# The FFN of a hybrid diffusion block on one Trainium2 core: the order of the seven block products of a tile, the copies of products ahead on ScalarE, activations stored whole and split when they are read, and x_mix stored one tile later

## Chip, core and metric

One core of a Trainium2 chip runs the whole layer as one program. The metric is the device time of one execution in microseconds (us); lower is better. TensorE (PE) multiplies, VectorE (DVE), ScalarE (ACT) and GpSimd (POOL) do elementwise work, and SyncE (SP) issues the DMAs. Each engine runs its own instructions strictly in order and waits on semaphores for the others. A matmul here multiplies a 128x128 weight block with 128x512 activations.

## The reference, cut to what matters

One layer over 1024 latent tokens of width 1024 with 256 context tokens: modulated RMSNorm, one input projection, three token mixers, a gated merge, and then the part that the change touches:

```python
x_mix = x + m_lat[:, :, 2] * merge_branches(ya, yb, yc, gates, w_branch[l], w_out[l])
h = rms_norm(x_mix, norm_ffn[l]) * (1.0 + m_lat[:, :, 4]) + m_lat[:, :, 3]
x = x_mix + m_lat[:, :, 5] * conv_ffn(h, w_up[l], w_dw[l], b_dw[l], w_down[l])
...
def conv_ffn(h, w_up, w_dw, b_dw, w_down):
    a, g = jnp.split(dwconv(h @ w_up, w_dw, b_dw), 2, axis=-1)   # width 2*2816, 3 taps along the tokens
    return (a * jax.nn.silu(g)) @ w_down
```

All of it is fp32 in and out.

## The kernel before, in words

**Precision.** A product of fp32 matrices is made of three fp32r matmuls: both operands are split into a high part (a cast to fp32r, on ACT) and a low part (the value less its high part, on DVE), and high x high, high x low and low x high are summed in PSUM. The helper `split` (L644) writes such a pair. Weights come in through raw buffers `wr` (3), high parts `wh` (3) and low parts `wl` (3).

**The stages at the end of the program.** `wo_half` (L656) is the output projection, half of the tokens at a time; it makes `xm` (x_mix), stores it to the DRAM tensor `xm_d` (L669) and sums its squares. Then the up projection runs over 22 tiles f of 128 hidden channels; each tile has a value half a and a gate half g. Tiles 0 and 1 are plain products (`plain`). While they run, the operand sums for the other tiles, T1 to T4, are built from `xm` and split (L742 to L757); eight of those sums run on POOL (L748, L752). Tiles 2 to 21 use a Strassen-Winograd scheme: the 2x2 block product (input halves by token halves) with 7 block products in place of 8, 12 matmuls each, 84 in a tile. `w_pair` (L764) loads and splits the weights of a tile, `w_sums` (L778) forms their sums S1 to S4 on POOL and splits them, `up_first` (L804) makes the first two products into the PSUM tile z, and `up_rest` (L812) the other five.

**One tile in up_rest.** The first product, z[:,0], is wanted by itself and as the start of a sum, so ACT copies it to `sn` (p, L815) before PE adds S2·T2 on top of it in the same bank; that sum is copied as u2 (L830). The products S3·T3 (bank c) and S1·T1 (bank d) are likewise copied as p7 (L825) and p5 (L826) before PE adds 22·T4 and S4·22 on top. POOL adds p7 and p5 (L831); DVE makes the four quadrants (L822, L832 to L834). `act_out` (L680) applies the convolution (ACT L692, then DVE L698 and L701, for the gate and for the value), SiLU on ACT (L705), and the product (L708), splits the result into ah and al and stores both parts to `act_d` with two DMAs (L713).

**The down projection** (from L848). Per token half tb and half of the output channels, PE goes through the 22 tiles f: 12 matmuls for each f (`dn`, L863). `act` (L854) loads the split activations, high and low part side by side, from `act_d` into a ring of 27 buffers `ac` (L859). The weights come as 11 units, each for two f.

**What sets the order.** A scheduler places every engine's instructions by program order, dependencies and priorities (`tc.high_priority` moves a piece ahead). The order on each engine is fixed when the program is built. Buffer counts (tag c: NC = 6; s12 and s34: 1) add waits of their own: a buffer is written again only when its last reader is done.

Of the kernel before, what the change touches and what calls it, by code (L numbers as in the profile page):

```python
# [9 lines left out]
F32 = mybir.dt.float32  # L10
F32R = mybir.dt.float32r
# [7 lines left out]
P = 128  # L19
# [15 lines left out]
SKEW = (1, 1)  # L35
APRIO = 60

NC = 6

LAST = (384, 128)  # L40
LPRIO = 40
# [49 lines left out]
def build(tc, ins, out, dbg=None):  # L91
    nc = tc.nc
    V, A, G, T, SP = nc.vector, nc.scalar, nc.gpsimd, nc.tensor, nc.sync
    with ExitStack() as top:
# [18 lines left out]
        def dt_(shape, name, dt=F32):  # L113
            return dp.tile(shape, dt, tag=name, name=name)
# [39 lines left out]
        kv_d = [dt_([10, P, 256], f"kv_d{b}") for b in range(2)]  # L154
        gate_d = dt_([3, KT, P, L], "gate_d")
        xm_d = dt_([2, KT, P, L // 2], "xm_d")
        act_d = dt_([FT, 2, P, 2, L // 2], "act_d")
        y_d = dt_([3, 4, P, L], "y_d")


# [463 lines left out]
        cw = tp.tile([P, 2 * FT, 4], F32, tag="cw", name="cw")  # L624
        SP.dma_start(cw, ins["conv"])

        for nm in ("T1", "T2", "T3"):
            blk[nm] = tuple(tp.tile([P, KQ, LH], F32R, tag=f"{nm}{p}", name=f"{nm}{p}") for p in "hl")
        ffs = ExitStack()
        ff = Aligned(ffs.enter_context(tc.tile_pool(name="ff", bufs=2, reuse_waits="tile")))  # L630
# [24 lines left out]
        def wo_half(hf):  # L655

            cols = slice(hf * LH, hf * LH + LH)
            ss = []
            for i in range(KT):
                w = w_unit(ins["w_out"][i], KT, P)  # L660
                z = bank("b", f"wo{hf}{i}", (P, 512))
                for k2 in range(2):
                    gemm_cm(z, [p[:, k2 * KQ:(k2 + 1) * KQ] for p in w], blk["12"[k2] + "12"[hf]], slice(0, LH),
                            first=k2 == 0, last=k2 == 1)
                xr = ff.tile([P, 512], F32, tag="o", name=f"xr{hf}{i}", bufs=2)
                SP.dma_start(xr, ins["xT"][i * P:(i + 1) * P, cols])
                V.scalar_tensor_tensor(out=xm[i][:, cols], in0=z, scalar=mods[:, 0, i:i + 1], in1=xr,
                                       op0=ALU.mult, op1=ALU.add)
                SP.dma_start(xm_d[hf, i], xm[i][:, cols])  # L669
                sumsq(ff, ss, xm[i][:, cols], i, f"m{hf}", 512, 4)  # L670
            return rms_row(ff, ss, 512, f"m{hf}", "a")

        rp = wo_half(0)
# [9 lines left out]
        def act_out(f, cc_):  # L683

            us = []
            for s in (1, 0):
                c_ = s * FT + f
                u = pc.tile([P, L], F32, tag="c", name=f"u{f}{s}", bufs=NC)
                o = 0
                for z in cc_[s]:  # L690
                    n = z.shape[-1]
                    A.activation(u[:, o:o + n], z, AF.Identity, scale=cw[:, c_, 1:2], bias=cw[:, c_, 3:4])  # L692
                    o += n
                o = 0
                for z in cc_[s]:
                    n = z.shape[-1]
                    e = min(n, L - 1 - o)
                    V.scalar_tensor_tensor(out=u[:, o + 1:o + 1 + e], in0=z[:, :e], scalar=cw[:, c_, 0:1],  # L698
                                           in1=u[:, o + 1:o + 1 + e], op0=ALU.mult, op1=ALU.add)
                    e = 0 if o else 1  # L700
                    V.scalar_tensor_tensor(out=u[:, o + e - 1:o + n - 1], in0=z[:, e:], scalar=cw[:, c_, 2:3],  # L701
                                           in1=u[:, o + e - 1:o + n - 1], op0=ALU.mult, op1=ALU.add)
                    o += n
                if s:
                    A.activation(u, u, AF.Silu)  # L705
                us.append(u)
            g_, a_ = us
            V.tensor_tensor(out=a_, in0=a_, in1=g_, op=ALU.mult)  # L708
            ah = pc.tile([P, L], F32R, tag="c", name=f"ah{f}", bufs=NC)
            al = pc.tile([P, L], F32R, tag="c", name=f"al{f}", bufs=NC)  # L710
            split((ah, al), a_)
            for j, t in enumerate((ah, al)):
                SP.dma_start(act_d[f].rearrange("b p j t -> p j b t")[:, j],  # L713
                             t.bitcast(F32).rearrange("p (b t) -> p b t", b=2))

        def plain(zs, ws, hf, ks):

# [16 lines left out]
        plain([z[:, 1] for z in za], ws, 1, range(KT))  # L734
        act_out(0, [[z.rearrange("p a b -> p (a b)")] for z in za])
        ws = up_units(1)
        za = [[bank(t, f"up1{s}{hf}", (P, LH)) for hf in range(2)] for s, t in enumerate("ab")]
        for s in range(2):
            for hf in range(2):
                plain([za[s][hf]], [ws[s]], hf, range(KT))  # L740

        t1, t2 = slice(0, LH), slice(LH, L)  # L742
        for k in range(KQ):
            h1, h2 = xm[k], xm[k + KQ]
            b = {nm: [p[:, k] for p in blk[nm]] for nm in ("T1", "T2", "T3")}
            V.tensor_tensor(out=h1[:, t1], in0=h1[:, t2], in1=h1[:, t1], op=ALU.subtract)
            split(b["T1"], h1[:, t1])
            G.tensor_tensor(out=h1[:, t2], in0=h2[:, t2], in1=h1[:, t2], op=ALU.subtract)  # L748
            split(b["T3"], h1[:, t2])
            V.tensor_tensor(out=h2[:, t2], in0=h2[:, t2], in1=h1[:, t1], op=ALU.subtract)  # L750
            split(b["T2"], h2[:, t2])
            G.tensor_tensor(out=h2[:, t1], in0=h2[:, t1], in1=h2[:, t2], op=ALU.subtract)  # L752
        act_out(1, za)

        blk["T4"] = blk["12"]
# [55 lines left out]

        def up_rest(f, z, w):  # L812
            p1 = P1[0]
            sn = p1.tile([P, LH], F32, tag="sn", name=f"p1_{f}", bufs=2)
            A.copy(sn, z[:, 0])  # L815
            prod(z[:, 0], w["S2"], blk["T2"], first=False)
            c = bank("a", f"upc{f}", (P, LH))
            prod(c, w["S3"], blk["T3"])
            d = bank("b", f"upd{f}", (P, LH))
            prod(d, w["S1"], blk["T1"])  # L820
            ca, cg = (pc.tile([P, L], F32, tag="c", name=f"c{s}{f}", bufs=NC) for s in range(2))
            V.tensor_tensor(out=ca[:, t1], in0=z[:, 1], in1=sn, op=ALU.add)  # L822
            p5 = ca[:, t2]
            p7 = cg[:, t2]
            A.copy(p7, c)  # L825
            A.copy(p5, d)  # L826
            prod(c, w["22"], blk["T4"], first=False)
            prod(d, w["S4"], blk["22"], first=False)
            u2 = p1.tile([P, LH], F32, tag="sn", name=f"u2_{f}", bufs=2)
            A.copy(u2, z[:, 0])  # L830
            G.tensor_tensor(out=cg[:, t2], in0=p7, in1=p5, op=ALU.add)  # L831
            V.tensor_tensor(out=cg[:, t2], in0=cg[:, t2], in1=u2, op=ALU.add)  # L832
            V.tensor_tensor(out=cg[:, t1], in0=c, in1=u2, op=ALU.add)  # L833
# [13 lines left out]

        pa = Aligned(top.enter_context(tc.tile_pool(name="pa", bufs=1, side="right", reuse_waits="tile")))  # L848
        p2 = Aligned(top.enter_context(tc.tile_pool(name="p2", bufs=1, reuse_waits="tile")))
        NRING = 27  # L850
        NRIGHT = 16
        acts = {}

        def act(tb, f):  # L854
            if (tb, f) not in acts:
                j = (tb * FT + f) % NRING
                t = (pa if j < NRIGHT else p2).tile([P, 2, LH], F32, tag=f"ac{j}", name=f"ac{tb}_{f}")
                with tc.high_priority(offset=APRIO):
                    SP.dma_start(t, act_d[f, tb])  # L859
                acts[tb, f] = tuple(t[:, j].bitcast(F32R) for j in range(2))  # L860
            return acts[tb, f]

        def dn(z, w, c, h, s, e):  # L863
# [629 lines left out]
```

## Time and profile before

| what | us |
|---|---|
| median of 3 runs (lowest, highest) | 2213.57 (2213.42, 2218.39) |
| the profiled execution's own time | 2217.27 |
| its span in the profile | 2215.5 |
| PE busy in the span | 2100.2 (95%) |
| DVE, ACT, POOL busy | 1465.1, 1002.2, 463.5 |

A row of the timeline gives the start, the duration, the engine, the source line, the operation and its tiles (buffer numbers left out), and in brackets how long the engine sat idle before it and who released it. Matmuls overlap, so PE counts as busy when it starts one each 0.23 us and each lasts 0.39 us; a wait of PE shows as a gap between two starts. PEclk is the granted share of TensorE's full clock. Times are from the start of the span; the up projection of tiles 2 to 21 runs from 1527 to 1946 us.

### The profile page before, as it was taken

Reading aid. Unit: us, or ns where it says so; the run is one execution under the profiler, and the core shown is the slowest. Engines: PE = TensorE matmul, PEld = TensorE weight load, DVE = VectorE, ACT = ScalarE, POOL = GpSimd, SP = SyncE. Lnnn points to the kernel's source line nnn. Section 1 sums busy time; section 2 is a strip of 40 time slices with the busy share of each in tenths; the row PEclk is TensorE's granted clock in tenths of the full one; section 3 lists DMA queues with packets and bytes.
Section 4 is the critical chain, followed back from the end, with each engine's and each line's share of the span. In section 5 each row is a group of like instructions: output and inputs, shape, how many; then the busy total and the mean of one; then the engine's idle time right before and its main releaser. Section 6 shows DMA issues by size and latency. Waiting matters only on the chain. (4 is left out here: it accounts for less than half of the span.)

```text
span 2215.5 us, 31104 instructions
## 1 busy us (share of the span) xinstructions
PE 2100.2 (95%) x11690; PEld 1739.3 (79%) x11690; DVE 1465.1 (66%) x2563; ACT 1002.2 (45%) x1789; POOL 463.5 (21%) x398
## 2 busy tenths in 40 slices
PE   7789999999999999999999999998999999999997
PEld 3778788789988888877777788877777777778887
DVE  6946566637565778599999757569777777732233
ACT  4523333311122777677777634355445445422222
POOL 1420010000021222133323100115443343200010
PEclk9999999999999999999999999999999999999999
DMA  7420111126644211211000454541333223297442
GB/s 307 128 66 30 49 39 34 53 97 190 200 141 128 88 45 51 89 34 32 32 32 27 145 180 150 165 143 67 105 111 108 96 105 105 90 351 281 161 126 91
DMA packets 102871, 247.67 MB, mean 112 GB/s; under 512 B 10944, under 2 KB 36032, under 8 KB 101696
## 3 DMA queue, kind: packets, MB, share of 16 engines
q1 hardware_dynamic: 102432, 245.62, 33.1%
q8 instruction: 92, 1.51, 0.3%
q14 instruction: 59, 0.48, 0.1%
q10 hardware_dynamic: 288, 0.07, 0.0%
HBM read 188.49 MB, written 57.15 MB: 111 GB/s over the span
## 5 line engine op out<-in xcount | busy, mean ns | idle before, releaser
L175 DVE TENSOR_TENSOR wl<-wr,wh 128x1024 fp32r<-128x1024 f32 x147 | 185.2, 1261 | 285.0 <-ACT wh L174 283.4
L174 ACT CAST wh<-wr 128x1024 fp32r<-128x1024 f32 x152 | 158.5, 1044 | 456.5 <-PE dn L865 109.7
L1236 DVE TENSOR_TENSOR pl<-pp,ph 128x512 fp32r<-128x512 f32 x236 | 158.7, 683 | 9.7 <-ACT ph L1235 8.4
L189 PE MATMUL gz<-hh,wh 128*128 128x512 f32 x384 | 156.4, 408 | 3.6 <-ACT gs L486 3.6
L1235 ACT CAST ph<-pp 128x512 fp32r<-128x512 f32 x236 | 136.1, 584 | 43.6 <-PE pp L1231 40.4
L191 PE MATMUL gz<-hh,wl 128*128 128x512 f32 x384 | 151.8, 396 | 0.0
L190 PE MATMUL gz<-hl,wh 128*128 128x512 f32 x384 | 151.6, 395 | 0.0
L200 PE MATMUL tm<-wl,hh 128*128 128x256 f32 x384 | 108.9, 284 | 2.3 <-DVE wl L175 2.3
L199 PE MATMUL tm<-wh,hh 128*128 128x256 f32 x384 | 108.7, 283 | 0.0
L201 PE MATMUL tm<-wh,hl 128*128 128x256 f32 x384 | 108.7, 283 | 0.0
L864 PE MATMUL dn<-ac,wh 128*128 128x512 f32 x264 | 104.0, 394 | 4.5 <-DMA ac<-act_d 4.5
L1225 PE MATMUL po<-ph,VHL 128*128 128x512 f32 x236 | 105.0, 445 | 1.3 <-ACT ph L1235 1.3
L1226 PE MATMUL po<-pl,VHL 128*128 128x512 f32 x236 | 98.9, 419 | 7.6 <-DVE pl L1236 7.3
L866 PE MATMUL dn<-ac,wl 128*128 128x512 f32 x264 | 103.5, 392 | 0.0
L865 PE MATMUL dn<-ac,wh 128*128 128x512 f32 x264 | 103.3, 391 | 0.0
L692 ACT ACTIVATE u<-c,cw 128x1024 f32<-128x1024 f32 x40 | 49.8, 1246 | 96.8 <-DVE c L833 64.8
L1231 PEld LDWEIGHTS pp<-ident,plat 128*128 128x128 f32 x512 | 61.2, 140 | 34.4 <-DVE pl L1236 22.0
L1231 PE MATMUL pp<-ident,plat 128*128 128x128 f32 x512 | 78.2, 275 | 10.3 <-DVE pl L1236 10.1
L189 PEld LDWEIGHTS gz<-hh,wh 128*128 128x128 f32 x384 | 72.8, 189 | 17.8 <-ACT gs L486 5.7
L783 POOL TENSOR_TENSOR s<-wr 128x512 f32<-128x512 f32 x20 | 42.6, 2128 | 200.7 <-DVE ws12l L646 11.5
L191 PEld LDWEIGHTS gz<-hh,wl 128*128 128x128 f32 x384 | 72.5, 189 | 15.3
L190 PEld LDWEIGHTS gz<-hl,wh 128*128 128x128 f32 x384 | 72.8, 190 | 11.5
(1496 smaller groups left out, 6286.3 us busy)
## 6 DMA issues: line engine op xcount, KB each, us to landing
wr<-in_w_cm SPq DMA_DIRECT2D x56, 512.0 KB, 3.6
wr<-in_w_up SPq DMA_DIRECT2D x44, 512.0 KB, 3.5
ac<-act_d SPq DMA_DIRECT2D x44, 512.0 KB, 6.2
wr<-in_w_down SPq DMA_DIRECT2D x33, 512.0 KB, 3.8
wmr<-in_w_mod SPq DMA_DIRECT2D x32, 512.0 KB, 4.8
gate_d<-gs SPq DMA_DIRECT2D x48, 256.0 KB, 2.3
sgt<-gate_d SPq DMA_DIRECT2D x24, 512.0 KB, 3.3
act_d<-ah SPq DMA_DIRECT2D x22, 512.0 KB, 2.9
```

Source lines behind the costliest of these rows:

```text
L174: A.copy(hi[:, :n], raw[:, :n])
L175: (lo_eng or V).tensor_tensor(out=lo[:, :n], in0=raw[:, :n], in1=hi[:, :n].bitcast(F32), op=ALU.subtract)
L189: T.matmul(psl, wh[:, k, c], hh[:, k0 + k, cols], start=s, stop=False)
L190: T.matmul(psl, wh[:, k, c], hl[:, k0 + k, cols], start=False, stop=False)
L191: T.matmul(psl, wl[:, k, c], hh[:, k0 + k, cols], start=False, stop=e)
L199: T.matmul(psl, hh[:, k, toks], wh[:, k % 4, :], start=s, stop=False)
L200: T.matmul(psl, hh[:, k, toks], wl[:, k % 4, :], start=False, stop=False)
L201: T.matmul(psl, hl[:, k, toks], wh[:, k % 4, :], start=False, stop=e)
L1225: T.matmul(po, vv, ph, start=n == 0, stop=False)
L1231: T.transpose(pp[:, h], PT(h, n), ident)
L1235: A.copy(ph, pp)
L1236: V.tensor_tensor(out=pl, in0=pp, in1=ph.bitcast(F32), op=ALU.subtract)
```

## The change

In `up_rest` the seven products come in the order z0, z1, S3·T3, S1·T1, S2·T2, 22·T4, S4·22; the four copies go through `keep`, with a scheduling priority of 30. `act_out` stores the fp32 activations once, whole, and `act` loads half a row set of 128x512 into one of four buffers `st` and splits it there into the ring, which has 25 places. The eight POOL sums go to DVE. Tile 1 makes its gate first. Tag c has 5 buffers. T3 is the first of the T tiles in its pool. The store of `xm` for tile i is written after the sum for tile i+1. The first activation load is written ahead of the loop over tb.

```diff
-NC = 6
+NC = 5
+KPRIO = 30
...
-        act_d = dt_([FT, 2, P, 2, L // 2], "act_d")
+        act_d = dt_([FT, P, L], "act_d")
...
-        for nm in ("T1", "T2", "T3"):
+        for nm in ("T3", "T1", "T2"):
...
-                SP.dma_start(xm_d[hf, i], xm[i][:, cols])
+                if i > 0:
+                    SP.dma_start(xm_d[hf, i - 1], xm[i - 1][:, cols])
...
+            SP.dma_start(xm_d[hf, KT - 1], xm[KT - 1][:, cols])
...
-            ah = pc.tile([P, L], F32R, tag="c", name=f"ah{f}", bufs=NC)
-            al = pc.tile([P, L], F32R, tag="c", name=f"al{f}", bufs=NC)
-            split((ah, al), a_)
-            for j, t in enumerate((ah, al)):
-                SP.dma_start(act_d[f].rearrange("b p j t -> p j b t")[:, j],
-                             t.bitcast(F32).rearrange("p (b t) -> p b t", b=2))
+            SP.dma_start(act_d[f], a_)
...
-        za = [[bank(t, f"up1{s}{hf}", (P, LH)) for hf in range(2)] for s, t in enumerate("ab")]
-        for s in range(2):
+        za = [[bank(t, f"up1{s}{hf}", (P, LH)) for hf in range(2)] for s, t in enumerate("ba")]
+        for s in (1, 0):
...
-            G.tensor_tensor(out=h1[:, t2], in0=h2[:, t2], in1=h1[:, t2], op=ALU.subtract)
+            V.tensor_tensor(out=h1[:, t2], in0=h2[:, t2], in1=h1[:, t2], op=ALU.subtract)
...
-            G.tensor_tensor(out=h2[:, t1], in0=h2[:, t1], in1=h2[:, t2], op=ALU.subtract)
+            V.tensor_tensor(out=h2[:, t1], in0=h2[:, t1], in1=h2[:, t2], op=ALU.subtract)
...
+            def keep(out, src):
+                with tc.high_priority(offset=KPRIO):
+                    A.copy(out, src)
+
             sn = p1.tile([P, LH], F32, tag="sn", name=f"p1_{f}", bufs=2)
-            A.copy(sn, z[:, 0])
-            prod(z[:, 0], w["S2"], blk["T2"], first=False)
+            keep(sn, z[:, 0])
             c = bank("a", f"upc{f}", (P, LH))
             prod(c, w["S3"], blk["T3"])
+            keep(p7, c)
+            V.tensor_tensor(out=ca[:, t1], in0=z[:, 1], in1=sn, op=ALU.add)
             d = bank("b", f"upd{f}", (P, LH))
             prod(d, w["S1"], blk["T1"])
...
+            keep(p5, d)
+            prod(z[:, 0], w["S2"], blk["T2"], first=False)
+            u2 = p1.tile([P, LH], F32, tag="sn", name=f"u2_{f}", bufs=2)
+            keep(u2, z[:, 0])
             prod(c, w["22"], blk["T4"], first=False)
             prod(d, w["S4"], blk["22"], first=False)
...
-        NRING = 27
+        NRING = 25
...
-                t = (pa if j < NRIGHT else p2).tile([P, 2, LH], F32, tag=f"ac{j}", name=f"ac{tb}_{f}")
+                t = (pa if j < NRIGHT else p2).tile([P, 2, LH], F32R, tag=f"ac{j}", name=f"ac{tb}_{f}")
                 with tc.high_priority(offset=APRIO):
-                    SP.dma_start(t, act_d[f, tb])
-                acts[tb, f] = tuple(t[:, j].bitcast(F32R) for j in range(2))
+                    raw = p2.tile([P, LH], F32, tag="st", name=f"st{tb}_{f}", bufs=4)
+                    SP.dma_start(raw, act_d[f][:, tb * LH:(tb + 1) * LH])
+                    acts[tb, f] = (t[:, 0], t[:, 1])
+                    split(acts[tb, f], raw)
...
+        act(0, 0)
```

Every later line has a number of its own in the changed file. On ACT, in tile 10 as in every tile from 4 to 19, these instructions stood in a row before (ws11h and vhS_11 are high parts of the weight sums of tile 11, wa12h of the weights of tile 12; p, u and c are the copies of products):

```order
L705 ACTIVATE u_16085<-u_16085 128x1024
L645 CAST ws11h<-s_11_16255 128x1024
L815 COPY p_10_16156<-up_16131 128x512
L645 CAST ah_16095<-u_16090 128x1024
L830 COPY u_10_16225<-up_16131 128x512
L645 CAST vhS_11_16273<-s_11_16256 128x512
L825 COPY c_16197<-upc_16170 128x512
L645 CAST wa12h<-wr_16393 128x1024
L826 COPY c_16196<-upd_16183 128x512
```

On ACT at the same place now:

```order
L708 ACTIVATE u_16040<-u_16040 128x1024
L646 CAST ws11h<-s_11_16200 128x1024
L818 COPY p_10_16108<-up_16081 128x512
L646 CAST vhS_11_16218<-s_11_16201 128x512
L818 COPY c_16107<-upc_16110 128x512
L818 COPY c_16106<-upd_16125 128x512
L646 CAST wa12h<-wr_16333 128x1024
L818 COPY u_10_16151<-up_16081 128x512
```

The cast ah is gone, the copies of c and d stand ahead of wa12h, and u, which is now made later by PE, stands behind it; p is still behind ws11h.

On DVE in the same tile, before (al is the low part of the activations, ws11l of the weight sums):

```order
L708 TENSOR_TENSOR u_16090<-u_16090,u_16085 128x1024
L646 TENSOR_TENSOR ws11l<-s_11_16255,ws11h 128x1024
L646 TENSOR_TENSOR al_16096<-u_16090,ah_16095 128x1024
L822 TENSOR_TENSOR c_16196<-up_16131,p_10_16156 128x512
L646 TENSOR_TENSOR vlS_11_16274<-s_11_16256,vhS_11_16273 128x512
L646 TENSOR_TENSOR wa12l<-wr_16393,wa12h 128x1024
L832 TENSOR_TENSOR c_16197<-c_16197,u_10_16225 128x512
```

And on DVE now:

```order
L711 TENSOR_TENSOR u_16045<-u_16045,u_16040 128x1024
L647 TENSOR_TENSOR ws11l<-s_11_16200,ws11h 128x1024
L825 TENSOR_TENSOR c_16106<-up_16081,p_10_16108 128x512
L647 TENSOR_TENSOR vlS_11_16219<-s_11_16201,vhS_11_16218 128x512
L647 TENSOR_TENSOR wa12l<-wr_16333,wa12h 128x1024
L835 TENSOR_TENSOR c_16107<-c_16107,u_10_16151 128x512
```

Only al has gone; POOL's five instructions of a tile stand in one and the same order in both.

On SP, where the up projection ends and the down projection begins, before (ah_17847 and al_17848 are tile 21's activations, ac_0 to ac_8 the ring, xt the loads of x_mix):

```order
L171 DMA wr_18044<-in_w_down 128x1024
L859 DMA ac_0_17880<-act_d 128x1024
L859 DMA ac_1_17894<-act_d 128x1024
L859 DMA ac_2_17914<-act_d 128x1024
L859 DMA ac_3_17928<-act_d 128x1024
L859 DMA ac_4_17948<-act_d 128x1024
L713 DMA act_d<-ah_17847 128x2x512
L713 DMA act_d<-al_17848 128x2x512
L859 DMA ac_5_17962<-act_d 128x1024
L859 DMA ac_6_17982<-act_d 128x1024
L893 DMA xt_17863<-xm_d 128x512 x8
```

And on SP now (u_17737 is tile 21's activations):

```order
L172 DMA wr_17964<-in_w_down 128x1024
L712 DMA act_d<-u_17737 128x1024
L865 DMA st_0_17754<-act_d 128x512
L865 DMA st_1_17788<-act_d 128x512
L865 DMA st_2_17811<-act_d 128x512
L865 DMA st_3_17828<-act_d 128x512
L901 DMA xt_17758<-xm_d 128x512
L865 DMA st_4_17851<-act_d 128x512
L901 DMA xt_17758<-xm_d 128x512 x7
L865 DMA st_5_17868<-act_d 128x512
```

Five activation loads stood ahead of the last tile's stores; now the first load stands behind the last tile's store. In the stretch of `wo_half`, the DMAs on SP (weights, xr, xm_d) stand in the same sequence in both programs.

## Rows read from the trace of the kernel before

**Rows 1.** The windows view: the first 50 us of the down projection. Columns: busy us of PE, PEld (weight load), DVE, ACT and POOL with the number of instructions, granted clock, share of the DMA engines, GB/s.
```profile
1950.00:2000.00 50.00, 47.33 (x201) 38.36 (x200) 14.73 (x13) 10.53 (x11) 0.00 (x0) 0.97 0.87 335
```

**Rows 2.** The view of waits of PE between 1540 and 1940 us (the wait for c in tile 2, 0.7 us, left out): who was waited for, us in total, times, longest.
```profile
PE up L801 <- ACT p L815: 22.0, 18, 2.4
PE upc L801 <- ACT vhS L645: 6.7, 1, 6.7
```

**Rows 3.** The timeline of PE in tile 10: its first matmul, and the two around the wait.
```profile
1701.60 0.39 PE L801 MATMUL up<-B11h,wa10h 128*128 128x512 f32 x1
...
1708.40 0.39 PE L801 MATMUL upc<-T3h,vhS 128*128 128x512 f32 x1
1709.94 0.50 PE L801 MATMUL up<-T2h,ws10h 128*128 128x512 f32 x1 [1.16 <-ACT p L815]
```

**Rows 4.** The timeline of ACT in tile 10: the cast of the weight sums, the copy p, the cast ah, and the cast of S4 (vhS).
```profile
1708.38 1.03 ACT L645 CAST ws11h<-s 128x1024 fp32r<-128x1024 f32 x1
1709.31 0.58 ACT L815 COPY p<-up 128x512 f32<-128x512 f32 x1
1711.80 1.05 ACT L645 CAST ah<-u 128x1024 fp32r<-128x1024 f32 x1 [1.91 <-DVE u L708]
...
1715.23 0.62 ACT L645 CAST vhS<-s 128x512 fp32r<-128x512 f32 x1
```

**Rows 5.** The timeline of DVE from one low part of the weight sums (ws11l) to the next (ws12l).
```profile
1711.68 1.22 DVE L646 TENSOR_TENSOR ws11l<-s,ws11h 128x1024 fp32r<-128x1024 f32 x1
1712.88 1.23 DVE L646 TENSOR_TENSOR al<-u,ah 128x1024 fp32r<-128x1024 f32 x1
...
1715.88 1.30 DVE L646 TENSOR_TENSOR vlS<-s,vhS 128x512 fp32r<-128x512 f32 x1 [1.17 <-ACT vhS L645]
1717.71 1.93 DVE L646 TENSOR_TENSOR wa12l<-wr,wa12h 128x1024 fp32r<-128x1024 f32 x1 [0.52 <-ACT wa12h L645]
1722.07 0.69 DVE L832 TENSOR_TENSOR c<-c,u 128x512 f32<-128x512 f32 x1 [2.43 <-POOL c L831]
...
1732.18 1.22 DVE L646 TENSOR_TENSOR ws12l<-s,ws12h 128x1024 fp32r<-128x1024 f32 x1
```

**Rows 6.** The timeline of POOL in the same stretch.
```profile
1713.03 2.23 POOL L783 TENSOR_TENSOR s<-wr 128x512 f32<-128x512 f32 x1 [11.49 <-DVE ws11l L646]
1715.35 1.29 POOL L784 TENSOR_TENSOR s<-s,wr 128x512 f32<-128x512 f32 x1
1717.27 1.29 POOL L789 TENSOR_TENSOR s<-wr,wr 128x512 f32<-128x512 f32 x1 [0.63 <-DVE vlS L646]
1718.52 2.27 POOL L790 TENSOR_TENSOR s<-wr,s 128x512 f32<-128x512 f32 x1
1720.75 1.28 POOL L831 TENSOR_TENSOR c<-c,c 128x512 f32<-128x512 f32 x1
```

**Rows 7.** The chain that ended last, followed back through 1700 to 1725 us: shares of that stretch by engine and line.
```profile
by line: POOL s L790 17.9%; DVE u L698 15.1%; DVE u L701 10.3%; POOL c L831 10.0%; ACT u L692 10.0%; issue 9.5%; DVE c L832 5.5%; DVE vlS L646 5.3%; POOL s L789 5.2%; DVE c L833 4.9%; DVE ws11l L646 4.9%; DVE al L646 4.8%; ACT vhS L645 2.5%
```

**Rows 8.** The timeline of PE at the start of tile 2: the last matmul of the first two products, the one behind the wait, and the end of the slower matmuls that follow.
```profile
1532.34 0.39 PE L803 MATMUL up<-B21h,wa2l 128*128 128x512 f32 x1
1539.44 0.80 PE L801 MATMUL upc<-T3h,vhS 128*128 128x512 f32 x1 [6.72 <-ACT vhS L645]
...
1545.66 0.39 PE L803 MATMUL up<-T2h,ws2l 128*128 128x512 f32 x1
```

**Rows 9.** The timelines of DVE, where the T tiles are built, and of ACT at the start of tile 2.
```profile
1503.28 1.77 DVE L646 TENSOR_TENSOR T2l<-xm,T2h 128x512 fp32r<-128x512 f32 x1
...
1530.83 0.79 ACT L692 ACTIVATE u<-up,cw 128x512 f32<-128x512 f32 x1
1537.34 1.06 ACT L705 ACTIVATE u<-u 128x1024 f32<-128x1024 f32 x1 [5.73 <-DVE u L701]
```

**Rows 10.** The timeline of PE: the last matmul ahead of the wait for p in tiles 4 and 20, and the last matmul of tile 21 with the first of the down projection.
```profile
1585.48 0.39 PE L801 MATMUL upc<-T3h,vhS 128*128 128x512 f32 x1
...
1913.66 0.39 PE L801 MATMUL upc<-T3h,vhS 128*128 128x512 f32 x1
...
1946.01 0.39 PE L803 MATMUL upd<-B22h,vlS 128*128 128x512 f32 x1
1948.27 0.50 PE L864 MATMUL dn<-ac,wh 128*128 128x512 f32 x1 [1.87 <-DMA ac<-act_d]
```

**Rows 11.** The timeline of DVE at the end of tile 21: the quadrant that the gate starts from, and the last product.
```profile
1944.87 0.68 DVE L833 TENSOR_TENSOR c<-upc,u 128x512 f32<-128x512 f32 x1
...
1952.89 1.23 DVE L708 TENSOR_TENSOR u<-u,u 128x1024 f32<-128x1024 f32 x1
```

**Rows 12.** The timeline of PE in the first tiles of the down projection: a wait for an activation load, and the matmuls behind it.
```profile
1967.96 0.39 PE L866 MATMUL dn<-ac,wl 128*128 128x512 f32 x1
1970.57 0.50 PE L864 MATMUL dn<-ac,wh 128*128 128x512 f32 x1 [2.22 <-DMA ac<-act_d]
...
1975.48 0.39 PE L866 MATMUL dn<-ac,wl 128*128 128x512 f32 x1
```

**Rows 13.** DMA issues: KB of each and median us from issue to landing, for the stores of activations and the loads of x by half rows.
```profile
act_d<-ah SPq DMA_DIRECT2D x22, 512.0 KB, 2.9
...
xr<-in_xT SPq DMA_DIRECT2D x16, 256.0 KB, 3.3
```

**Rows 14.** Time from issue to landing, least, median and most, of the ring loads ac.
```profile
DMA to landing us min/median/max: 4.5/6.2/10.6
```

More of the change, by code (lines that the diff above doesn't have):

```diff
@@ L813, in up_rest @@
             p1 = P1[0]
+            ca, cg = (pc.tile([P, L], F32, tag="c", name=f"c{s}{f}", bufs=NC) for s in range(2))
+            p5 = ca[:, t2]
+            p7 = cg[:, t2]
+            def keep(out, src):
+                with tc.high_priority(offset=KPRIO):
+                    A.copy(out, src)
             sn = p1.tile([P, LH], F32, tag="sn", name=f"p1_{f}", bufs=2)
-            A.copy(sn, z[:, 0])
-            prod(z[:, 0], w["S2"], blk["T2"], first=False)
+            keep(sn, z[:, 0])
             c = bank("a", f"upc{f}", (P, LH))
             prod(c, w["S3"], blk["T3"])
+            keep(p7, c)
+            V.tensor_tensor(out=ca[:, t1], in0=z[:, 1], in1=sn, op=ALU.add)
             d = bank("b", f"upd{f}", (P, LH))
             prod(d, w["S1"], blk["T1"])
[L821 to L826, printed above, removed]
+            keep(p5, d)
+            prod(z[:, 0], w["S2"], blk["T2"], first=False)
+            u2 = p1.tile([P, LH], F32, tag="sn", name=f"u2_{f}", bufs=2)
+            keep(u2, z[:, 0])
             prod(c, w["22"], blk["T4"], first=False)
             prod(d, w["S4"], blk["22"], first=False)
-            u2 = p1.tile([P, LH], F32, tag="sn", name=f"u2_{f}", bufs=2)
-            A.copy(u2, z[:, 0])
             G.tensor_tensor(out=cg[:, t2], in0=p7, in1=p5, op=ALU.add)
@@ L855, in act @@
             if (tb, f) not in acts:
-                j = (tb * FT + f) % NRING
-                t = (pa if j < NRIGHT else p2).tile([P, 2, LH], F32, tag=f"ac{j}", name=f"ac{tb}_{f}")
+                n = tb * FT + f
+                j = n % NRING
+                t = (pa if j < NRIGHT else p2).tile([P, 2, LH], F32R, tag=f"ac{j}", name=f"ac{tb}_{f}")
                 with tc.high_priority(offset=APRIO):
-                    SP.dma_start(t, act_d[f, tb])
-                acts[tb, f] = tuple(t[:, j].bitcast(F32R) for j in range(2))
+                    raw = p2.tile([P, LH], F32, tag="st", name=f"st{tb}_{f}", bufs=4)
+                    SP.dma_start(raw, act_d[f][:, tb * LH:(tb + 1) * LH])
+                    acts[tb, f] = (t[:, 0], t[:, 1])
+                    split(acts[tb, f], raw)
             return acts[tb, f]
```

## The prediction

> **What bounds the kernel now.** I read the waits of PE first. In the up projection PE waits 18 times for ACT's copy p, 22.0 us in all, and once 6.7 us for a weight cast [rows 2]. So PE is the engine that loses time; the question is what makes p late. The timeline of PE gives the pitch: 30 matmuls from 1701.60 to 1708.40, 0.2267 us each, and then a gap in front of the first matmul that needs p [rows 3]. From the seventh S3·T3 matmul of tile 4 to that of tile 20 are 328.18 us [rows 10], 20.51 us a tile, where 84 matmuls need 84 x 0.2267 = 19.04.
>
> ACT shows why p is late: it stands behind the cast ws11h [rows 4], which stands behind the post-processing of the tile before. The chain of waits through 1700 to 1725 us then shows what really paces a tile: there is POOL, DVE and ACT in it and no PE [rows 7]. It is a loop. When ws11l ends on DVE (1712.90), POOL may write the weight sums of the next tile, five instructions from 1713.03 to 1722.03 [rows 6]; the last is the sum p7+p5, for which L832 waits; L832, the convolution and the product follow on DVE and ACT up to ws12l, 20.50 us after ws11l [rows 5]. POOL and DVE hardly overlap in it: POOL's L783 takes 2.23 us where L784 takes 1.29, and al runs on DVE meanwhile; DVE's vlS and wa12l take 1.30 and 1.93 beside L784 and L789, where ws11l of the same width as wa12l takes 1.22 [rows 5, 6]. So PE's wait for p is the sign, and this loop is the bound.
>
> The Trainium skill (SBUF — State Buffer, "Practical consequences" in its part on the shared pair) says that a DVE instruction with two SBUF inputs and a GpSimd instruction that reads SBUF exclude each other, whoever issues first. The trace agrees (2.23 against 1.29 us). By that rule a new order inside the loop saves nothing and only work taken out counts; without it the loop would end below 19.04 and PE would set the pace, which is rival A.
>
> **The sum before.** Tile 2's first matmul starts 23 x 0.2267 before 1532.34, at 1527.13; tile 21's last at 1946.01 [rows 8, 10]. 1679 steps of 0.2267 are 380.6 us, 418.9 were taken: 38.3 us lost. Of these, 6.9 is the wait in tile 2 (7.10 less one step) and 2.8 the slow matmuls behind it (15 steps in 6.22 us instead of 3.40: the lower of the two clock levels) [rows 8]; 328.2 - 16 x 19.04 = 23.5 is tiles 4 to 19; 5.1 is the rest of tiles 2, 3 and 20.
>
> **Part by part.** *No split in act_out.* Every tile loses ah (1.05 on ACT) and al (1.2 on DVE, start to start) [rows 4, 5]. ACT is idle 1.91 us ahead of ah, so its loss is worth nothing by itself. al lies in the loop. It cannot give less than what it adds to L783, 2.23 - 1.29 = 0.94, nor more than its own 1.2; vlS no longer queues behind it and u on ACT, so I take 1.1. The loop becomes 20.5 - 1.1 = 19.4, still 0.36 above PE.
>
> *The order of the products.* S2·T2 comes after S1·T1, so PE needs p 24 matmuls (5.4 us) after z, not 7; the waits for p go, as far as the loop lets them. What is late next is the loop itself, 0.36 us a tile; PE meets it again at p, after the little lead that the new order gives. In 17 tiles (4 to 20): 6.1 us lost instead of 23.5 and tile 20's share. I count no gain for the order beyond that. The copies of c and d stand ahead of wa12h, which needs S2·T2 done anyway: nothing. Tag c with 5 buffers adds a wait: copy c overwrites what the value's convolution of the tile before reads, which is done before ws11l starts (1711.68). The copy's turn is after p and vhS, 1709.9 + 0.6, so ACT waits 1.2 us at most, with d, wa12h and u behind it; PE wants c only after 12 more matmuls (2.7 us): nothing.
>
> *Tiles 1 and 2.* vhS, for which PE waited 6.7 us, stands behind the SiLU of tile 1, which waited 5.73 for DVE [rows 2, 9]. Now the gate is made first, 48 matmuls (10.9 us) ahead of tile 1's end, and vhS follows the last convolution start: 1527.3 + 0.79 + 0.62 = 1528.7, its low part some 2.8 later (three half-tile steps of 0.7 and itself); PE needs that at 1533. The eight sums moved to DVE cost 8 x 0.68 = 5.4 there, but a DVE instruction next to a POOL sum takes 1.77 instead of 0.68 [rows 9], 1.1 each, and two al (2.4) go: a gain on DVE, not a loss. I take 1.0 us lost in tiles 2 and 3 together; bounds 0 and what is lost today. Total lost 7.1, so the up projection **gains 31.2 us**.
>
> *x_mix.* In the order SP's sequence is the same in `wo_half`: nothing either way.
>
> *Stores and loads.* act_d is written once and read in half the bytes. The splits come back in the down projection: per f a cast of 0.62 and a subtraction of 0.68, with half a weight unit (0.52 and 0.61) 1.15 on ACT and 1.3 on DVE against 12 x 0.2267 = 2.72 on PE; both engines are mostly idle there [rows 1]. PE hides them, except for the first f.
>
> *The seam.* Today five loads stand ahead of tile 21's stores on SP, and PE starts the down projection 2.26 us after tile 21's last matmul [rows 10]. Now the first load stands behind tile 21's store. That store waits for the product: from L833 to the end of L708 are 9.25 us [rows 11], and L833 can start when 22·T4 is done, 12 steps less 0.4 before the last matmul's start (-2.25; it was -1.1), so the product is ready at +7.0, and store and load are issued one behind the other. The load's landing takes 2.9 to 6.2 us (a 512 KB store; the ring loads' median); the nearest row is xr, 256 KB in half rows, 3.3; I take 4.0, since the store is in flight ahead of it [rows 13, 14]. Cast 0.62: first matmul at +11.6, 11.4 us lost. After 6.7 us of idleness the clock cost 2.8 [rows 8]; I take that again: 14.2. Today the same stretch loses 2.0 at the start, 2.4 in a later wait for a load and 1.7 behind it (14 steps in 4.91 us instead of 3.17) [rows 10, 12]: 6.1. Those waits go with half the bytes. The seam **costs 8.1 us** more.
>
> Sum: -31.2 + 8.1 = -23.1. Against the profiled execution (2217.27, span 2215.5) that is 2194.2; that one lies 3.7 above the median of the runs shown, so against 2213.57 I predict **2190.5**. Its own bounds: al 0.94 to 1.2 (2.7 us up, 1.7 down), landing 2.9 to 6.2 (-1.1, +2.2), tiles 2 and 3 up to 4 more: 2188 to 2199.
>
> **Rivals.** *A. PE becomes the bound* at 19.04 a tile, if the loop falls below that. For: vlS's cast stands ahead of the copies now. Against: POOL's and DVE's instructions still exclude each other. Lost 1.0 instead of 7.1: 2184.5.
>
> *B. The wait at tile 2 stays*, since DVE has 5.4 us more and is full there. Against: the stretched rows [rows 9]. 9.7 comes back: 2200.
>
> *C. Slower: the down projection starves.* Four raw buffers, and a load waits on SP for the split of the fourth before it, with weight loads behind it. A round is 6.2 + 0.62 + 0.68 = 7.5 us for four f, which PE uses in 10.9; the longest landing, 10.6 [rows 14], makes 11.9 and a wait. A wait costs 2.4 + 1.7 = 4.1 us with the clock [rows 12]. Six such waits cancel the gain; from eight on the kernel is slower by over 0.3%. Every second f of the first pass, eleven, would give 2236. Against: half the bytes. The Trainium skill (Perfetto Trace Analysis, "DMA Optimizations") speaks for it: runs of 2 KB instead of 4 KB move less per time. The row for such runs here, xr, is not slow (3.3 us for 256 KB).
>
> *D. Little is left:* B, with two to four waits of C: 2208 to 2217.
>
> **How the numbers follow.** Chances: forecast 0.52, A 0.16, B 0.17, D 0.08, C 0.07. The likeliest gives 2190.5. The range 2178 to 2206 holds the forecast, A and B with their bounds and leaves out C and D. A difference of 0.3% (6.6 us) is about what a measurement of this kernel tells from none: faster 0.85, same 0.08, slower 0.07.
>
> **What would show it.** The steps between the same matmuls of tiles 4 and 20: 19.4 us (19.04 speaks for A, 20 or more against the loop). POOL's L783 near 1.3 us. No wait of PE over 2 us in tile 2. One gap of 11 to 12 us between tile 21 and the down projection, slow matmuls behind it, and then no wait for loads. Wrong would be: the loop as long as before though al is gone, or waits of PE for `ac` all through the first pass.

## The result and the profile after

| | median us | range, runs | profiled execution, span |
|---|---|---|---|
| before | 2213.49 | 2212.89 to 2218.39, 4 | 2217.27, 2215.5 |
| after | 2192.26 | 2190.67 to 2193.44, 4 | 2193.44, 2191.7 |

After over before is 0.9899, with a 95% interval of 0.9882 to 0.9916: 21.2 us less, where 2190.5 was forecast.

The waits of PE between 1530 and 1930 us, to be held against [rows 2]: the 18 waits for p and the one for vhS are gone. What is left is the seam (the passage from tile 21 to the down projection), and small waits for L825, the sum z1+p on DVE.

```profile
PE dn L871 <- ACT ac L646: 11.8, 1, 11.8
PE up L799 <- DVE c L825: 3.3, 3, 1.6
```

The timeline of DVE over one round, from ws11l to ws12l, answers to [rows 5]; that of POOL in the same stretch to [rows 6].

```profile
1694.19 1.22 DVE L647 TENSOR_TENSOR ws11l<-s,ws11h 128x1024 fp32r<-128x1024 f32 x1
1695.33 0.68 DVE L825 TENSOR_TENSOR c<-up,p 128x512 f32<-128x512 f32 x1
1695.93 1.45 DVE L647 TENSOR_TENSOR vlS<-s,vhS 128x512 fp32r<-128x512 f32 x1
1699.97 2.15 DVE L647 TENSOR_TENSOR wa12l<-wr,wa12h 128x1024 fp32r<-128x1024 f32 x1 [2.59 <-ACT wa12h L646]
1703.30 0.69 DVE L835 TENSOR_TENSOR c<-c,u 128x512 f32<-128x512 f32 x1 [1.18 <-POOL c L834]
...
1713.40 1.22 DVE L647 TENSOR_TENSOR ws12l<-s,ws12h 128x1024 fp32r<-128x1024 f32 x1
```

```profile
1695.54 1.29 POOL L781 TENSOR_TENSOR s<-wr 128x512 f32<-128x512 f32 x1 [11.49 <-DVE ws11l L647]
1696.91 1.62 POOL L782 TENSOR_TENSOR s<-s,wr 128x512 f32<-128x512 f32 x1
1698.49 1.29 POOL L787 TENSOR_TENSOR s<-wr,wr 128x512 f32<-128x512 f32 x1
1699.74 1.29 POOL L788 TENSOR_TENSOR s<-wr,s 128x512 f32<-128x512 f32 x1
1700.99 2.27 POOL L834 TENSOR_TENSOR c<-c,c 128x512 f32<-128x512 f32 x1
```

The round is 1713.40 - 1694.19 = 19.21 us instead of 20.50. POOL's first sum takes 1.29 instead of 2.23 us, since al no longer runs beside it, and the gap of 0.63 us ahead of the third sum is gone.

The chain of waits through 1685 to 1710 us holds PE alone, where [rows 7] held no PE:

```profile
by line: PE up L799 18.6%; PE up L800 18.2%; PE up L801 18.1%; PE upd L800 8.2%; PE upc L799 8.2%; PE upd L801 8.1%; PE upc L800 7.3%; PE upd L799 7.3%; PE upc L801 7.2%
```

That reads as if PE set the pace now. It doesn't yet: 84 matmuls need 19.04 us. The missing 0.17 us a tile are split over short steps at the first S2·T2 matmul (1696.06 to 1696.41), too short to be listed as a wait (the run e10_sum_dve settles this).

The timeline of PE from tile 21 into the down projection answers to the last two rows of [rows 10]:

```profile
1915.35 0.39 PE L801 MATMUL upd<-B22h,vlS 128*128 128x512 f32 x1
1927.56 0.80 PE L871 MATMUL dn<-ac,wh 128*128 128x512 f32 x1 [11.82 <-ACT ac L646]
1928.29 0.79 PE L872 MATMUL dn<-ac,wh 128*128 128x512 f32 x1
...
1931.87 0.50 PE L871 MATMUL dn<-ac,wh 128*128 128x512 f32 x1
1932.20 0.39 PE L872 MATMUL dn<-ac,wh 128*128 128x512 f32 x1
```

The timelines of DVE, SP and ACT there, in this order: the product, the store and the loads behind it, the first casts.

```profile
1921.08 1.22 DVE L711 TENSOR_TENSOR u<-u,u 128x1024 f32<-128x1024 f32 x1
...
1922.33 0.33 SPq L712 DMA_DIRECT2D act_d<-u  x1
1922.75 2.20 SPq L865 DMA_DIRECT2D st<-act_d  x4
...
1926.89 1.26 ACT L646 CAST ac<-st 128x512 fp32r<-128x512 f32 x2 [7.54 <-DMA st<-act_d]
```

The product is ready 6.95 us after the last matmul's start, the first load's cast begins 4.1 us after its issue, the first matmul comes at +12.2: one line of waiting, link by link. From 1915.35 to 1932.20 are eleven steps, 2.5 us at 0.2267; they took 16.85, so the seam loses 14.4 us. Later in the down projection PE waits for no load.

### The profile page after: what moved, and what is told of

Its sections match the earlier page's. It is cut to its first block, busy times and chain, and to the rows that moved or that the text cites. A ratio compares the mean times of both kernels' runs of the same rounds, so it can differ in the third digit from the quotient of the medians.

```text
span 2191.7 us, 31143 instructions
## 1 busy us (share of the span) xinstructions
PE 2095.4 (96%) x11690; PEld 1737.6 (79%) x11690; DVE 1467.9 (67%) x2593; ACT 1007.5 (46%) x1811; POOL 440.4 (20%) x390
## 5 line engine op out<-in xcount | busy, mean ns | idle before, releaser
L871 PE MATMUL dn<-ac,wh 128*128 128x512 f32 x264 | 103.9, 393 | 11.8 <-ACT ac L646 11.8
L191 PEld LDWEIGHTS gz<-hl,wh 128*128 128x128 f32 x384 | 72.8, 190 | 11.6
L781 POOL TENSOR_TENSOR s<-wr 128x512 f32<-128x512 f32 x20 | 30.7, 1534 | 231.7 <-DVE ws2l L647 21.5
```

The lines of the kernel that those rows point to most:

```text
L191: T.matmul(psl, wh[:, k, c], hl[:, k0 + k, cols], start=False, stop=False)
L871: T.matmul(z, w[0][:, c], h[0], start=s, stop=False)
```

## The experiments

Each kernel was timed beside the kernel before, whose medians were 2212.6 to 2213.4 in these runs. "Ratio" is to the kernel before, with its 95% interval. A median holds the whole program, also parts that no change here touches: in these traces the 500th matmul starts between 104.1 and 107.8 us, and the last one of `wo_half` between 1476.4 and 1482.3. So the last column gives, from the one trace of each run, the time from the last matmul of `wo_half` to the end of the span; it is 735.0 us in the kernel before and 711.3 in the changed kernel.

| run | median us, runs | ratio | round us | behind `wo_half` us |
|---|---|---|---|---|
| e1_order_alone | 2207.79, 10 | 0.9976 (0.9967 to 0.9986) | 20.13 | 726.2 |
| e2_whole_alone | 2202.31, 6 | 0.9956 (0.9942 to 0.9969) | 19.57 | 723.2 |
| e3_dve_op | 2207.11, 10 | 0.9971 (0.9962 to 0.9981) | 20.08 | 725.3 |
| e4_act_op | 2192.03, 4 | 0.9906 (0.9891 to 0.9920) | | 710.3 |
| e5_gate_last | 2193.36, 4 | 0.9911 (0.9896 to 0.9926) | | 713.9 |
| e7_sums_pool | 2197.95, 4 | 0.9931 (0.9916 to 0.9946) | | 717.5 |
| e6_xm_now | 2190.85, 4 | 0.9902 (0.9887 to 0.9917) | | 710.5 |
| e8_seam_cw | 2185.39, 4 | 0.9876 (0.9860 to 0.9893) | | 706.8 |
| e9_seam_early | 2185.31, 4 | 0.9879 (0.9864 to 0.9894) | | 704.4 |
| e10_sum_dve | 2181.63, 4 | 0.9862 (0.9847 to 0.9876) | 19.04 | 703.0 |
| e12_seam_pool | 2183.32, 4 | 0.9861 (0.9842 to 0.9880) | | 703.5 |
| e13_first_pool | 2177.22, 5 | 0.9833 (0.9819 to 0.9846) | | 698.0 |

### What paces a tile

The theory: the loop ws_l, POOL's five instructions, convolution, product, ws_l. The rival: PE asked for p too early, and the new order of the products gave the gain.

**e1_order_alone**: the kernel before with the change's `up_rest` (the new order and `keep`), nothing else.

> The kernel before, with only the new order of the block products and the early copies on ScalarE; the split in act_out, its two stores, six buffers of tag c and the old loads stay. Loop theory (a tile lasts as long as the round ws_l, POOL sums, convolution, product, ws_l, and al stands in that round): the round stays at 20.3 to 20.5 us, PE's wait only moves to another matmul, and the median falls by 0 to 6 us, to 2207 to 2213. Rival (PE lost its time because it asked for the copy p 7 matmuls after z, and the new order mended that): the tile falls to 19.1 to 19.4 us and the median by 20 to 30, to 2183 to 2193.

5.6 us less: the theory's branch by the median, but the round of 20.13 lies below the 20.3 that it allowed, so the order does give something in the loop. PE's wait moved, as expected: from p to later copies on ACT (L821, 8.9 us in 11 waits) and to L828, this kernel's sum z1+p (8.8 us in 6). The wait of 6.7 us for vhS in tile 2 stands unchanged. Its timeline of POOL, and of DVE at both ends:

```profile
1688.14 2.21 POOL L784 TENSOR_TENSOR s<-wr 128x512 f32<-128x512 f32 x1 [11.49 <-DVE ws10l L647]
1690.43 1.62 POOL L785 TENSOR_TENSOR s<-s,wr 128x512 f32<-128x512 f32 x1
1692.01 1.29 POOL L790 TENSOR_TENSOR s<-wr,wr 128x512 f32<-128x512 f32 x1
...
1686.79 1.22 DVE L647 TENSOR_TENSOR ws10l<-s,ws10h 128x1024 fp32r<-128x1024 f32 x1
...
1706.92 1.22 DVE L647 TENSOR_TENSOR ws11l<-s,ws11h 128x1024 fp32r<-128x1024 f32 x1
```

The first sum still collides with al (2.21), but the third follows without the gap of 0.63 us of [rows 6].

**e2_whole_alone**: the changed kernel with the old `up_rest`, nothing else.

> The changed kernel with the old order of the block products and the old places of the copies; whole store, split when read and all the rest stay. Loop theory: without al the round is 19.2 to 19.5 us whatever the order of the products, but PE asks for p after 7 matmuls instead of 24 and the copies wait longer, so some tenths per tile may come back: 0 to 8 us above the changed kernel, 2192 to 2200. Rival (the order gave the gain): the tile is at 20 us or more, 15 to 25 us above the changed kernel, 2207 to 2217.

10 us above the changed kernel by the median, 12.0 by the last column: between the two branches. Its timelines, as in e1:

```profile
1700.02 1.29 POOL L781 TENSOR_TENSOR s<-wr 128x512 f32<-128x512 f32 x1 [11.49 <-DVE ws11l L647]
1701.39 1.30 POOL L782 TENSOR_TENSOR s<-s,wr 128x512 f32<-128x512 f32 x1
1703.32 1.30 POOL L787 TENSOR_TENSOR s<-wr,wr 128x512 f32<-128x512 f32 x1 [0.63 <-DVE vlS L647]
...
1698.67 1.22 DVE L647 TENSOR_TENSOR ws11l<-s,ws11h 128x1024 fp32r<-128x1024 f32 x1
...
1718.24 1.22 DVE L647 TENSOR_TENSOR ws12l<-s,ws12h 128x1024 fp32r<-128x1024 f32 x1
```

Here the collision is gone and the gap is back. So each half of the change shortened the same stretch of POOL, in a different place. The round of five kernels, cut at the same three events:

| us | before | e1 | e2 | after | e3 |
|---|---|---|---|---|---|
| ws_l starts to POOL's first sum | 1.35 | 1.35 | 1.35 | 1.35 | 1.36 |
| that to DVE's first step that needs POOL's fifth | 9.04 | 8.68 | 8.11 | 7.76 | 8.61 |
| that to the next ws_l | 10.11 | 10.10 | 10.11 | 10.10 | 10.11 |
| round | 20.50 | 20.13 | 19.57 | 19.21 | 20.08 |

Only the middle line moves. Taking al out is worth 0.93 there (before to e2) or 0.92 (e1 to after); the order is worth 0.36 or 0.35; they add up. "The order" is here the whole new `up_rest`: the sequence of the products and the priority of the copies changed together, and neither was tried without the other. Over the 17 tiles the order's share in e2 is 6.0 us; longer waits in tiles 2 and 3 (6.2 us instead of 3.1, with slow matmuls behind the longest) and at the seam (12.6 instead of 11.8) make up the rest.

**e3_dve_op** and **e4_act_op**: a stand-in for al alone, and one for ah alone.

```diff
             SP.dma_start(act_d[f], a_)
+            if 2 <= f < FT - 1:      # e3; in e4: A.copy(g_, a_)
+                V.tensor_tensor(out=g_, in0=a_, in1=g_, op=ALU.subtract)
```

> The changed kernel with one more DVE instruction in tiles 2 to 20: a subtraction of the same width and the same two SBUF inputs as al, in the place that al had behind ws_l, into the dead gate tile; nothing is stored from it. Loop theory: 1.0 to 1.2 us in each of 19 tiles, the round from 19.2 to 20.2 to 20.4, POOL's first sum (L781 of the changed kernel) back from 1.29 to 2.2 us, 18 to 23 us above the changed kernel: 2210 to 2215. Rival (PE sets the pace of the changed kernel, or DVE's idle time swallows the instruction): 0 to 3 us.

14.9 us above the changed kernel, 17 x 0.87 = 14.8: the theory, its size taken too high (18 to 23). The first sum:

```profile
1681.82 2.14 POOL L783 TENSOR_TENSOR s<-wr 128x512 f32<-128x512 f32 x1 [11.49 <-DVE ws10l L647]
```

An instruction of 1.22 us on DVE costs 0.87 us, by making POOL wait: the length that it adds to its neighbour, not its own.

> The changed kernel with one more ACT instruction in tiles 2 to 20: a copy as wide as the cast ah that the change took out, behind the copy p, into the dead gate tile; nothing is stored from it. Loop theory: ACT has idle time there and the instruction is not in the round: within 2 us of the changed kernel, 2190 to 2195. Rival (ACT's queue, in which p stood behind other work, was the bound): 10 to 20 us more.

2192.03: an ACT instruction of the same width (1.05 us, in tiles 2 to 20) costs nothing, as the theory has it.

### The start of tile 2, and x_mix

**e5_gate_last** (tile 1's value half first again) and **e7_sums_pool** (the two sums of the T loop back on `G`) take one edit each out of the change.

> The changed kernel with the value half of tile 1 computed first again, as before (banks a, b and the order of s). By the prediction's step on tile 2 (the wait of 6.7 us went because the gate's SiLU no longer comes last): the wait at tile 2's third product comes back by 3 to 7 us, with the slow matmuls behind it 3 to 9 us above the changed kernel, 2195 to 2201. Rival (it went because DVE was relieved, of al twice and of waiting for POOL's sums): 0 to 2 us.

1.1 us more by the median, less than the two intervals can tell apart; 2.6 more by the last column. PE's waits in the first tiles:

```profile
PE up L799 <- DVE c L825: 4.8, 1, 4.8
PE upc L799 <- ACT vhS L646: 1.2, 1, 1.2
```

Of the 6.7 us for vhS only 1.2 are back, and tile 3's wait for L825 is 4.8 us instead of 1.5. The prediction's reason for tile 2, the gate made first, carries a small part of what was put on it.

> The changed kernel with the eight T sums that the change moved to DVE back on POOL. If DVE was held up by POOL's sums at tile 2 (1.77 us for an instruction that takes 0.68 alone): DVE comes 2 to 6 us later to tile 1's convolution and tile 2 waits that much longer, 2194 to 2200. If not: within 2 us of the changed kernel, or 1 to 3 faster since DVE has 8 x 0.68 us less to do.

5.7 us more (6.3 by the last column), in the first branch's range but not by its way: no wait for vhS came back. The timeline of ACT while the T tiles are built, and of PE behind it:

```profile
1504.80 0.62 ACT L646 CAST T3h<-xm 128x512 fp32r<-128x512 f32 x1 [2.23 <-POOL xm L746]
...
1508.77 1.04 ACT L175 CAST wh<-wr 128x1024 fp32r<-128x1024 f32 x1
...
1509.87 0.79 PE L190 MATMUL up<-B11h,wh 128*128 128x512 f32 x1 [3.61 <-ACT wh L175]
```

ACT waits for POOL's sums, and a weight cast that PE needs for tile 1's gate stands behind it: a place that the prediction did not name. The kernel before has this cast as late, and PE does not wait for it, since the value half comes first there:

```profile
1508.51 1.05 ACT L174 CAST wh<-wr 128x1024 fp32r<-128x1024 f32 x1
```

So the sums on DVE mend what the gate's new place would cost; e7 does not show that they gain anything over the kernel before.

**e6_xm_now**: each x_mix tile stored at once.

> The changed kernel with each x_mix tile stored at once again. By the prediction the store one tile later is worth nothing: within 1.5 us of the changed kernel, 2191 to 2194. Rival (the store held the next load of x on SP and with it the convolution input): 2 to 6 us more.

2190.85, no difference by the intervals (0.8 us less by the last column): worth nothing, as forecast.

### The seam, and a faster kernel

**e8_seam_cw**:

```diff
-            SP.dma_start(act_d[f], a_)
+            (G if f == FT - 1 else SP).dma_start(act_d[f], a_)
...
-        cw = tp.tile(...)    # ahead of T3, T1, T2; now behind them, so that st lies over T3
```

> The changed kernel with the seam mended: tile 21's activation store goes out on POOL's queue, and the table cw lies behind the T tiles in memory, so that the first loads of the down projection wait neither for that store nor for the last convolution. If the seam's 11.8 us are the load standing behind product and store: the loads land before tile 21 ends, the first split's low part still stands behind the product on DVE, so PE waits 7 to 8 us instead of 11.8, and the median falls by 3.5 to 5: 2187 to 2189. Rival (the memory or the queue holds the loads all the same): no change, 2192.

6.9 us less than the changed kernel by the median, 4.5 by the last column, which is the size expected; the rest lies, by the traces, ahead of the end of `wo_half`. PE's waits of the seam:

```profile
PE dn L871 <- ACT ac L646: 4.2, 1, 4.2
PE dn L872 <- DVE ac L647: 2.3, 1, 2.3
```

6.5 us instead of 11.8. So the load behind the product and the store was the seam's cause (the store's queue and the place of cw changed together); what is left is the cast behind ACT's SiLU and the low part behind DVE's product.

**e9_seam_early**: `st` in the pool `pa`, over B11.

> The kernel of e8_seam_cw with the raw buffers st at the base of the right side (over B11) instead of over T3. The loads can start sooner, and in the order DVE makes the low parts of the first three activations ahead of tile 21's product L711 instead of behind it. If PE's second wait of the seam (2.3 us for that low part in e8) hangs on DVE's queue: 1.0 to 1.3 us less, 2184 to 2185, the first wait of 4.2 us stays since ACT casts behind the SiLU. If it hangs on the loads' landing: no change, 2185.

The second wait fell from 2.3 to 0.5 us as the queue theory has it. The median is the same (2185.31), but the stretch behind tile 21's last matmul takes 269.5 us instead of 271.8, one trace each: the gain is in the seam, and the medians do not show it.

**e10_sum_dve**: e9 with `V` for `G` in the sum p7+p5.

> The kernel of e9_seam_early with the sum p7+p5 (the last of POOL's five instructions in the loop, 2.27 us there) on DVE. Loop theory: POOL's part of the round shrinks by 2.3 us and DVE's grows by 0.7, so the round would fall to 17.6 to 18, below the 19.04 us of PE's 84 matmuls: PE sets the pace at 19.04, 0.17 us a tile less, 3 to 4 us in all with tile 3's wait: 1 to 4 us below e9. Rival (the 0.17 is PE's own and the loop is no longer the bound of the changed kernel): no change against e9, or some tenths per tile slower for the added DVE work.

3.7 us less. DVE's timeline:

```profile
1690.80 1.22 DVE L647 TENSOR_TENSOR ws11l<-s,ws11h 128x1024 fp32r<-128x1024 f32 x1
...
1709.84 1.22 DVE L647 TENSOR_TENSOR ws12l<-s,ws12h 128x1024 fp32r<-128x1024 f32 x1
```

19.04, PE's 84 matmuls to the digit. So the loop still paced the changed kernel at 19.21, and now PE does. In the traces the up projection is 1.9 us shorter (385.7 instead of 387.6) and not 17 x 0.17 = 2.9: a wait of 2.7 us in tile 3 now has eight slow matmuls behind it, which take 1.6 us back.

**e12_seam_pool**: the first four loads on POOL's queue, the first two splits on POOL.

```diff
-                    SP.dma_start(raw, ...)
-                    split(acts[tb, f], raw)
+                    (G if n < 4 else SP).dma_start(raw, ...)
+                    if n < 2:
+                        G.tensor_copy(t[:, 0], raw)
+                        G.tensor_tensor(out=t[:, 1], in0=raw, in1=t[:, 0].bitcast(F32), op=ALU.subtract)
+                    else:
+                        split(acts[tb, f], raw)
```

> The kernel of e10_sum_dve with the first four activation loads of the down projection issued on POOL's queue, which is idle in tile 21, and the first two activations split by POOL (a cast and a subtraction each) instead of ACT and DVE, which are at tile 21's convolution then. If the seam is the queues (SP held by weight loads that wait for their slots, ACT by the SiLU, DVE by the product): both acts are split about when tile 21's last matmul ends, PE goes on with 0 to 1 us of wait, waits some 2 us for the third activation, and has few or no slow matmuls: 4 to 8 us below e10. If the copies of POOL are too slow or the loads land late: 0 to 3 us.

Not faster than e10 (1.7 us more by the median, 0.5 by the last column): nearest the second branch. POOL's timeline:

```profile
1903.24 0.80 POOL L865 DMA_DIRECT2D st<-act_d  x1 [32.43 <-DVE c L825]
1915.63 1.60 POOL L865 DMA_DIRECT2D st<-act_d  x3 [11.59 <-DVE c L837]
1917.23 0.97 POOL L868 CAST ac<-st 128x512 fp32r<-128x512 f32 x1
```

The first load was early. The second waited for memory that tile 21's last sum L837 still read, and the split of the first stood behind it on POOL's queue.

**e13_first_pool**: two loads only on POOL's queue, in raw buffers of their own over memory that is free early (`early`, in `pa`); the rest as in e8 and e10.

> The kernel of e8_seam_cw (raw buffers over T3) with the sum p7+p5 on DVE as in e10_sum_dve and, for the first two activations alone, raw buffers of their own over memory that tile 21 leaves free early, their loads on POOL's queue and their split on POOL. In e12_seam_pool three of the four loads stood on POOL's queue behind a buffer that tile 21's last sums still read (15.6 us of idle POOL shows as a wait of 11.6 for L837), so its split came late. If that was all that failed there: both activations are split before tile 21 ends, PE runs 24 matmuls (5.4 us) of the down projection without a wait, then waits about 3 us for the third one's low part, and the median is 3 to 6 below e10, 2176 to 2179. If POOL's split or its queue is slow by itself: within 2 us of e10, 2180 to 2184.

2177.22, the first branch. POOL's timeline, and PE's waits of the seam:

```profile
1900.40 0.62 POOL L868 CAST ac<-sa 128x512 fp32r<-128x512 f32 x1
1901.11 1.28 POOL L869 TENSOR_TENSOR ac<-sa,ac 128x512 fp32r<-128x512 f32 x1
1903.65 0.61 POOL L868 CAST ac<-sa 128x512 fp32r<-128x512 f32 x1 [1.26 <-DMA sa<-act_d]
1904.35 1.30 POOL L869 TENSOR_TENSOR ac<-sa,ac 128x512 fp32r<-128x512 f32 x1
```

```profile
PE dn L875 <- ACT ac L646: 1.4, 1, 1.4
PE dn L876 <- DVE ac L647: 0.8, 1, 0.8
```

Both splits are done before tile 21's last matmul (1909.88), and the seam's wait is 2.2 us. This kernel takes 0.9833 of the time before, 15 us less than the changed kernel (13.2 by the last column).

## Why the prediction was right, step by step

**The bound.** Right: al in the loop, not PE's early demand for p, held the tile (e1, e3, e4). POOL and DVE exclude each other as [rows 5, 6] said: POOL's first sum fell from 2.23 to 1.29. The Trainium skill (SBUF — State Buffer, "Who interferes with whom") states it for a DVE instruction with two SBUF inputs and a GpSimd instruction that reads SBUF, and e3 agrees (2.14 beside the added instruction). PE met the loop again, not at p, where it was forecast, but at L825, which stands behind ws_l on DVE.

**The size of the loop term, 20.5 - 1.1 = 19.4.** The result is 19.21, from two errors that went opposite ways. al was worth 0.93, the lower bound of 0.94 and not 1.1: what it adds to POOL's sum. The 0.16 put on top, for vlS leaving ACT's queue, did not come with al: in e2 the gap ahead of POOL's third sum is still 0.63. And "no gain for the order beyond that" was wrong: the order was worth 0.36. The prediction's rule, that only work taken out counts in the loop, overlooked that POOL idled 0.63 us in it, for vlS [rows 6]. ACT cast vhS behind the copy u, which waited 1.89 us for DVE's L822; in the new order that copy is elsewhere, vlS comes earlier, and POOL's gap turns into 0.33 us of collision (L782, 1.62 instead of 1.29). The copy u before, and vhS now, ahead of ws11l:

```profile
1714.74 0.59 ACT L830 COPY u<-up 128x512 f32<-128x512 f32 x1 [1.89 <-DVE c L822]
...
1693.37 0.62 ACT L646 CAST vhS<-s 128x512 fp32r<-128x512 f32 x1 [0.98 <-PE upc L800]
```

**Tiles 2 and 3.** 1.0 us was allowed; the two waits for L825 are 1.76 and 1.63 in excess of a step, 3.4. The wait of 6.7 us did go, as forecast, and vhS was cast at 1528.75 (1528.7 forecast). What took the wait away stays open: with the gate last 1.2 us of it are left (e5), with the sums on POOL nothing (e7), and without both edits and with al all of it (e1). So neither edit was needed by itself for most of it, and al's share in tiles 0 and 1 was not tried alone. The sums on DVE were needed for tile 1 (e7), of which the prediction had only DVE's side.

**The sum of the up projection.** Tile 2's first matmul now starts at 1527.68, tile 21's last at 1915.35: 387.7 us, so 7.1 lost and 31.2 gained, both to the digit as forecast. That is luck in part: 17 x 0.17 = 2.9 in the loop instead of 6.1, 3.4 in tiles 2 and 3 instead of 1.0, 0.8 in small steps (0.4 of it one longer step in tile 9). Of the whole program, the traces of before and after differ by 23.7 us behind `wo_half`, where 23.1 was forecast, and the medians by 21.2.

**The seam.** Product at +7.0 (6.95 measured), landing 4.0 behind it (4.6: 0.45 to the load's issue and 4.14 from there), first matmul at +11.6 (12.2), 14.2 us lost (14.4). From tile 21's last matmul to the end of the span the kernel takes 276.3 us instead of 269.5: 6.8 more, where 8.1 was forecast. 0.6 of the difference is a second wait for a load before (1961.78) that the prediction left out, and 0.5 lies behind the program's last down-projection matmul (13.0 us to the end instead of 13.5).

**Rivals.** A was off by little: the loop stayed 0.17 above PE. B did not come; C did not either: no wait for a load after the first. The Trainium skill (Perfetto Trace Analysis, "DMA Optimizations") let one fear short runs; here 44 loads in runs of 2 KB landed in 4.3 us (median, 256 KB). Before, 512 KB in runs of 4 KB took 6.2 [rows 14], so a load now moves less per time (60 KB per us instead of 83), in the page's direction; size and run changed together. But PE never waited for one but the first.

**x_mix** was worth nothing (e6). The five buffers of tag c, the 25 places of the ring and the place of the first load have no run of their own.

## What to carry to other kernels

Where two engines share a loop that is longer than TensorE's work, cut the round at fixed events and compare the pieces: here one piece of three held every gain, and the gains in it added up. An instruction in such a loop costs what it delays on the other engine, and an engine that waits inside the loop can be helped by order alone. When a phase ends in a store and the next begins with a load, look at which queue and which memory the first load stands behind: mending that took 9.7 us off the stretch behind tile 21's last matmul here (276.3 us in the changed kernel, 266.6 in e13_first_pool), nearly half of what the whole change gave, with no less work. And when a difference of medians is a few us, compare a stretch of the traces that holds only what was changed.

## What the runs showed of the hardware

TensorE's clock does not follow the length of a single wait alone. In e13_first_pool, idle stretches of 1.43 and 0.76 us with two matmuls between them came before a fall: the windows view has the clock at 1.00, 0.50 and 1.00 (2.4, 1.2 and 2.4 GHz) before, behind and later.

```profile
1910.00:1915.30 5.30, 5.30 (x25) 4.39 (x24) 5.08 (x5) 2.25 (x2) 0.00 (x0) 1.00 0.93 331
1918.63:1921.78 3.15, 3.15 (x7) 2.48 (x8) 1.15 (x2) 0.00 (x0) 0.00 (x0) 0.50 0.96 321
1922.20:1928.00 5.80, 5.80 (x27) 4.80 (x26) 1.64 (x2) 2.73 (x5) 0.00 (x0) 1.00 0.36 136
```

A single wait of 1.48 us in tile 3 of the changed kernel left it at 1.00, and so did one of 2.83 us in tile 2 of e7_sums_pool (1.00 from 1548.3 to 1553.0), while slow matmuls came behind the 2.22 us of [rows 12]. And the loss did not grow with the idleness: behind 11.8 us the ten steps from 1927.56 to 1932.20 took 4.64 us instead of 2.27, 2.4 more, where [rows 8] show 2.8 behind 6.7.
